# Gate products of seven mLSTM heads by Strassen's seven block products, in a part of their own

## The chip, the cores and the metric

The kernel runs on one core of a Trainium2 chip. The metric is device time in microseconds (us), the median of several executions. The core has a matrix engine (TensorE, PE in the profile), a vector engine (VectorE, DVE), a scalar engine (ScalarE, ACT), GpSimd (POOL), and a queue engine (SyncE, SP) that only issues transfers. Each works through its own list of instructions in order; semaphores connect them. Transfers run on 16 DMA engines that all queues share; here SP issues most of them, ACT and GpSimd a few.

## The reference, cut to what matters

A network of two layers works on 512 latent tokens and 256 context tokens, width 1024. Layer 0 mixes a long convolution with attention. Layer 1 is an mLSTM with 8 heads, and the change lies there. In short:

```
h            = rms_norm(x) * (1 + scale) + shift           # 768 x 1024
q, k, v, o, z, gates = split(h @ w_in)                     # per head: 128, 128, 256, 256, 256 columns
q, k         = silu(short_conv(q, k))
h_f, h_b     = chunkwise recurrence over q, k, v, gates, forward and backward
h            = rms_norm((h_f + h_b) * sigmoid(o), head_norm)
y            = (h * silu(z)) @ w_out                       # 512 latent tokens only
```

Of one head, o and z are needed for the 512 latent tokens alone, so their product is (512 x 1024) @ (1024 x 512). All numbers are fp32.

## The kernel before, in words

**Products.** The matrix engine takes a reduced fp32 form, so each fp32 operand is kept as two tiles, hi (a rounded copy, made by ACT) and lo (the rest, a subtraction on DVE). `split` (L1019) makes such a pair, and `mm3` (L1029) does one product as three matmuls: hi by hi, hi by lo, lo by hi. The activations of the layer lie in `hTh` and `hTl`, feature rows on the partitions, 8 feature tiles (`KT`) of 128 by 768 tokens. `load_w` (L1044) fetches a slice of 256 weight columns in two halves of 512 KB from SP into the three buffers `wr` and splits each half into `wh` and `wl`, which exist twice. `proj_tok` (L1196) then makes 128 tokens by 256 columns out of 8 x 3 = 24 matmuls; `proj_seg` (L1183) makes the transposed product for 512 or 256 tokens. Results lie in eight banks of PSUM, four called `pj`, four `pm`.

**Layer 1.** Head 0's values and the gate logits (`value`, L2347) come first, then `gates` (L2233), a chain of scans and exponentials on 64 rows, whose results `turn` (L2292) transposes. `head` (L2338) does a head: load the slice of q and k and that of v, project, convolve, apply silu (`conv_silu`, L2322), transpose the keys; then load the slices of o and z; then the recurrence over six chunks of 128 tokens, once forward and once backward (L2444 to L2504). Each step of the recurrence is a short chain: a matmul `pc`, an update of the state `C` on DVE, its split into `Ch` and `Cl`, a matmul with q, an addition on DVE. PE has other work in between: eight items, `out_gate` and `gate_z` (L2405 and L2411), 24 matmuls each, which `fill` places into the recurrence of the same head. `normed` and `result` (L2508 and L2521) finish a head and store it; they run inside the next one.

**The order.** Engine calls are not issued where they stand. `record` (L1004) collects them under a name, and `play` (L1009) issues them in the order that the table `ORDERS` gives for it, as numbers of recorded calls. What is issued so is pinned: every engine, SP and GpSimd included, goes through its calls in just this order (L1016, L1017). The parts that matter here are `l1a` (from head 0's values to `turn`) and `l1b` (the rest of layer 1, down to the first products of the output projection). `SLOTS` says in the same manner which buffer each tile takes. Nothing of `l1b` can be issued on an engine before its last call of `l1a`.

Of the kernel before, what the change touches and what calls it, by code (L numbers as in the profile page):

```python
# [7 lines left out]
F32 = mybir.dt.float32  # L8
# [6 lines left out]
P = 128  # L15
NL, NC, NT = 512, 256, 768
D = 1024
KT = 8
# [71 lines left out]
def _layout(i):  # L90
# [50 lines left out]
    o["head_norm"] = a["o_head_norm"][0].reshape(8, 1, 256)  # L141
# [10 lines left out]
class Ctx:  # L152
# [334 lines left out]
    ],  # L487
# [357 lines left out]
    ],  # L845
    "yraw@9": [
        1, 0, 0, 1, 1, 1, 0, 0,
    ],
    "ess@9": [
        0, 0, 0, 0, 0, 0,  # L850
# [1790 lines left out]
```

## Time and profile before

| | us |
|---|---|
| median of 3 runs (lowest, highest) | 1515.31 (1514.62, 1515.59) |
| the profiled execution | 1514.84 |
| its span, first to last instruction | 1513.1 |
| TensorE busy | 1480.6 |
| VectorE busy | 989.3 |
| ScalarE busy | 717.0 |
| GpSimd busy | 57.7 |

The span is what the profile shows; 1.74 us lie around it. A busy TensorE means that a matmul was under way; matmuls overlap, so a mean duration is longer than the distance from one start to the next. In groups and chains every instruction is put down to L1014, since the helper there issues all of them; the names of tiles tell them apart. In the rows of a window the columns are: the stretch, its length, busy time and number of instructions of PE, PEld, DVE, ACT and POOL, the granted TensorE clock, the busy share of the DMA engines, and GB/s.

### The profile page before, as it was taken

To read this page: it belongs to the slowest core of one execution; us is meant where nothing else is said; L and a number is where in the kernel's file an instruction comes from. 1 tells how busy PE (TensorE), PEld (TensorE's weight loads), DVE (VectorE), ACT (ScalarE), POOL (GpSimd) and SP (SyncE) were. 2 spreads that over 40 slices of the span, in tenths; PEclk is the share of its full clock that TensorE was granted. 3 is DMA by queue.
4 is the path that set the end of the run, shared out by engine and by line. 5 is a ranking of instruction groups with operands and counts; after the bars stand their busy time and mean duration, and the time that the engine had idled before them with its cause. 6 is when DMAs were issued, how large, how long until landed. Compare 5 with 4: busy or idle time off the path is not lost.

```text
span 1513.1 us, 25999 instructions
## 1 busy us (share of the span) xinstructions
PE 1480.6 (98%) x10542; PEld 1365.8 (90%) x10542; DVE 989.3 (65%) x1943; ACT 717.0 (47%) x1545; POOL 57.7 (4%) x97
## 2 busy tenths in 40 slices
PE   7999999999999999999999899999999999999997
PEld 5889999889999998989987789999999999999885
DVE  6688787887866666667236866666656575677435
ACT  6634344334434444445233667546354554546332
POOL 1000000000000000000000100000000000000000
PEclk9999999999999999999999999999999999999999
DMA  9411121221231111252643313131222323232741
GB/s 378 156 58 65 65 67 41 75 78 39 56 94 45 39 68 53 97 179 70 211 154 127 131 57 105 58 112 54 91 90 82 99 71 98 77 99 74 276 156 70
DMA packets 44815, 151.78 MB, mean 100 GB/s; under 512 B 5311, under 2 KB 7879, under 8 KB 42136
## 3 DMA queue, kind: packets, MB, share of 16 engines
q1 hardware_dynamic: 41448, 141.48, 28.2%
q0 software_dynamic: 1360, 6.42, 1.3%
q10 hardware_dynamic: 1888, 2.22, 0.5%
q8 instruction: 83, 1.36, 0.4%
q14 instruction: 36, 0.29, 0.1%
HBM read 135.39 MB, written 14.71 MB: 99 GB/s over the span
## 4 chain that ended last, share of the span: by engine, by line
PE 91%; DVE 3%; ACT 3%; issue 1%; DMA 1%; POOL 0%; SPq 0%; POOLq 0%; DVEq 0%; ACTq 0%
PE pj L1014 76%; PE pm L1014 13%; PE s L1014 3%; DVE wl L1014 0%; ACT hf L1014 0%; ACT wh L1014 0%; ACT q L1014 0%; DMA xt<-in_x 0%; DVE hf L1014 0%; DVE hh L1014 0%; DVE hTl L1014 0%; ACT wl L1014 0%; DVE yacc L1014 0%; DVE xt L1014 0%; ACT hTh L1014 0%
## 5 line engine op out<-in xcount | busy, mean ns | idle before, releaser
L1014 PE MATMUL pj<-wh,hTh 128*128 128x256 f32 (+2 forms) x1536 | 435.1, 289 | 5.1 <-ACT hTh L1014 1.9
L1014 PE MATMUL pj<-wl,hTh 128*128 128x256 f32 (+2 forms) x1536 | 433.0, 286 | 1.7 <-DVE wl L1014 1.7
L1014 PE MATMUL pj<-wh,hTl 128*128 128x256 f32 (+2 forms) x1536 | 430.1, 286 | 1.9 <-DVE hTl L1014 1.9
L1014 PEld LDWEIGHTS pj<-wh,hTh 128*128 128x128 f32 x1536 | 287.3, 189 | 12.0 <-ACT wh L1014 3.4
L1014 PEld LDWEIGHTS pj<-wl,hTh 128*128 128x128 f32 x1536 | 288.8, 189 | 4.8 <-DVE wl L1014 2.3
L1014 PEld LDWEIGHTS pj<-wh,hTl 128*128 128x128 f32 x1536 | 287.1, 189 | 4.2 <-DVE hTl L1014 2.1
L1014 PE MATMUL pj<-hTh,wh 128*128 128x512 f32 (+1 forms) x832 | 286.6, 345 | 0.0
L1014 PE MATMUL pj<-hTl,wh 128*128 128x512 f32 (+1 forms) x832 | 285.2, 343 | 0.6 <-DVE hTl L1014 0.6
L1014 PE MATMUL pj<-hTh,wl 128*128 128x512 f32 (+1 forms) x832 | 284.7, 343 | 0.0
L1014 DVE TENSOR_TENSOR wl<-wr,wh 128x1024 fp32r<-128x1024 f32 x149 | 180.5, 1214 | 75.0 <-ACT wh L1014 74.8
L1014 ACT CAST wh<-wr 128x1024 fp32r<-128x1024 f32 x149 | 154.2, 1044 | 81.6 <-PE pj L1014 41.9
L1014 PEld LDWEIGHTS pj<-hTh,wh 128*128 128x128 f32 x832 | 156.8, 188 | 18.5 <-ACT mrow L1014 0.4
L1014 PEld LDWEIGHTS pj<-hTh,wl 128*128 128x128 f32 x832 | 156.6, 188 | 18.7
L1014 PEld LDWEIGHTS pj<-hTl,wh 128*128 128x128 f32 x832 | 156.8, 188 | 17.9 <-DVE hTl L1014 0.9
L1014 DVE TENSOR_TENSOR PTl<-pj,PTh 128x384 fp32r<-128x384 f32 (+1 forms) x80 | 41.0, 525 | 21.5 <-ACT PTh L1014 21.4
L1014 ACT CAST PTh<-pj 128x384 fp32r<-128x384 f32 (+1 forms) x80 | 35.1, 459 | 41.1 <-PE pj L1014 38.7
L1014 DVE SCALAR_TENSOR_TENSOR C<-C,apb,pj 128x258 f32<-128x258 f32 x64 | 30.8, 481 | 33.7 <-PE pj L1014 27.5
L1014 DVE SCALAR_TENSOR_TENSOR cvo<-pj,cv,cvo 128x511 f32<-128x511 f32 (+1 forms) x48 | 31.2, 657 | 23.0 <-ACT cvo L1014 22.5
L1014 PE MATMUL pm<-Rh,dfa 128*128 128x256 f32 (+1 forms) x192 | 45.0, 305 | 0.0
L1014 DVE TENSOR_REDUCE mx<-s 128x1 f32<-128x768 f32 (+1 forms) x48 | 37.0, 773 | 11.2 <-PE s L1014 11.0
L1014 DVE TENSOR_TENSOR med<-big 128x512 f32<-128x512 f32 (+1 forms) x48 | 40.4, 865 | 5.0 <-ACT big L1014 4.8
L1014 PE MATMUL s<-dfa,qTh 128*128 128x256 f32 (+1 forms) x160 | 41.6, 342 | 1.3 <-ACT hdh L1014 1.3
(311 smaller groups left out, 2642.3 us busy)
## 6 DMA issues: line engine op xcount, KB each, us to landing
wr<-in_o_w_in SPq DMA_DIRECT2D x64, 512.0 KB, 4.8
wr<-in_e_w_in SPq DMA_DIRECT2D x52, 512.0 KB, 4.7
wh<-in_w_mod SPq DMA_DIRECT2D x18, 1024.0 KB, 5.1
wr<-in_e_w_out SPq DMA_DIRECT2D x16, 512.0 KB, 4.7
wr<-in_o_w_out SPq DMA_DIRECT2D x16, 512.0 KB, 6.6
xt<-in_x SPq DMA_DIRECT2D x12, 512.0 KB, 5.9
decay<-nc_scratch SPq DMA_DIRECT2D x16, 256.0 KB, 4.8
y_scratch<-y SPq DMA_DIRECT2D x8, 512.0 KB, 5.8
```

Source lines behind the costliest of these rows:

```text
L1014: x = fn(*a, **k)
```

## The change

For heads 0 to 6 the products for o and z move out of `head` into `l1a`, and are done by Strassen's scheme (Winograd's form). Of one head, the product (512 x 1024) @ (1024 x 512) is cut into 2 x 2 blocks: 256 tokens, 512 features, and o or z. Seven block products of 24 matmuls each take the place of eight. Five use sums of blocks:

- On the side of the activations the four forms `D1`, `F5`, `F6`, `F3` are made once for all heads: 4 additions of hi and lo (`whole`), 4 subtractions and 4 splits, each on 128 x 1024 numbers. Three products use plain blocks of `hTh` and `hTl`.
- On the side of the weights the sums are made anew for each head. A buffer `ch` (two exist) is loaded with one block and split; then GpSimd's queue issues a transfer that adds the next block to it, it is split again, and so on: four splits and three adding transfers, one after another. One more sum is made in a `wr` buffer (`r3`). So a head has 4 plain loads and 4 adding transfers of 512 KB, and 7 splits, where there were 4 loads and 4 splits.
- The results are put together on DVE and ACT, the tanh of both gates is applied, and the tiles are stored to DRAM (`ozd`), 512 KB each. The recurrence of the head loads them again, from SP.

The recurrence of head h now has the projections q, k and v of head h + 1 as its other work (`Head`); head 7 still has its own o and z, done the direct way. The multiplication of z by `head_norm` on DVE and the eight small loads of it on ACT's queue go; `result` scales by it while it copies out of PSUM. Tiles of `gates` share buffers with the new ones. The orders of `out0`, `l1a` and `l1b` and the slots are written anew.

The core of the diff:

```diff
+    A11, A12, A21, A22 = block(0, 0), block(0, 1), block(1, 0), block(1, 1)
+    a21, a11 = whole("zs", A21), whole("uu", A11)
+    V.tensor_tensor(a11, a21, a11, ALU.subtract)
+    D1 = form("d1", a11)
+    a22 = whole("so", A22)
+    V.tensor_tensor(a21, a21, a22, ALU.subtract)
+    F5 = form("f5", a21)
+    V.tensor_tensor(a22, a22, a11, ALU.subtract)
+    F6 = form("f6", a22)
+    a12 = whole("zs", A12)
+    V.tensor_tensor(a12, a12, a22, ALU.subtract)
+    F3 = form("f3", a12)
...
+    def product(ps, a, b):
+        for t in range(2):
+            for kt in range(4):
+                l = [x[:, kt, t * P:(t + 1) * P] for x in a]
+                out = ps[:, t * 256:(t + 1) * 256]
+                mm3(out, l, (b[0][:, kt], b[1][:, kt]), kt == 0, kt == 3)
+        return ps
+
+    def plus(raw, src):
+        G.dma_start(raw, src, accum_op=ALU.add)
...
+    def gates_oz(h):
+        o, z = ow[4 * h + 2], ow[4 * h + 3]
+        b11, b21, b12, b22 = o[:, 0:4], o[:, 4:8], z[:, 0:4], z[:, 4:8]
...
+        chain = raw_block(b11, "ch", 2, gp)
+        p1 = product(PJ(), A11, weights(chain))
+        S.copy(u, p1)
+        plus(chain, b12)
+        p2 = product(PM(), A12, weights(raw_block(b21)))
+        V.tensor_tensor(so[:, 0], p2, u, ALU.add)
+        S.activation(so[:, 0], so[:, 0], AF.Tanh, scale=0.5)
+        q5 = product(PJ(), F5, weights(chain))
+        plus(chain, b22)
+        r3 = raw_block(b12)
+        plus(r3, b22)
+        q7 = product(PM(), D1, weights(r3))
+        q6 = product(PJ(), F6, weights(chain))
+        plus(chain, b21)
+        V.tensor_tensor(u2, q6, u, ALU.subtract)
+        V.tensor_tensor(zs[:, 0], q5, u2, ALU.add)
+        V.tensor_tensor(u2, q7, u2, ALU.add)
+        V.tensor_tensor(zs[:, 1], q7, zs[:, 0], ALU.add)
+        q3 = product(PM(), F3, weights(raw_block(b22)))
+        V.tensor_tensor(zs[:, 0], q3, zs[:, 0], ALU.add)
+        q4 = product(PJ(), A22, weights(chain))
+        V.tensor_tensor(so[:, 1], q4, u2, ALU.subtract)
+        S.activation(so[:, 1], so[:, 1], AF.Tanh, scale=0.5)
+        for t in (1, 0):
+            th = T(gp, "gi", (P, 512))
+            S.activation(th, zs[:, t], AF.Tanh, scale=0.5)
+            V.scalar_tensor_tensor(zs[:, t], th, 1.0, zs[:, t], ALU.add, ALU.mult)
+        SP.dma_start(ozd[h, 0], so.rearrange("p t (i b) -> p (t i) b", b=256))
+        SP.dma_start(ozd[h, 1], zs.rearrange("p t (i b) -> p (t i) b", b=256))
+
+    for h in range(7):
+        gates_oz(h)
+        if h == 1:
+            turn()
+    play()
+    g1.close()
+    record("l1b")
...
+        if N:
+            N.load()
+            N.load_v()
+            SP.dma_start(so, ozd[h, 0])
+            SP.dma_start(zs, ozd[h, 1])
+            work = [(N.key, 0), (N.key, 1), (N.query,)] + [(N.value, i) for i in (4, 5, 0)] + [(N.turned,)] + [(N.value, i) for i in (1, 2, 3)]
...
-                S.copy(y[:, t], ps.rearrange("p n t -> p (n t)"))
+                S.activation(y[:, t], ps.rearrange("p n t -> p (n t)"), AF.Copy, scale=hnc[:, 2 * h + t:2 * h + t + 1])
```

In the new order of `l1a` the last calls are head 6's product `q4` (24 matmuls), then the subtraction that gives `so[:, 1]` (call 1708), its tanh (1709) and the store of `so` (1714). The new order of `l1b` begins with four of the five copies `ka` of head 0's first direction on ACT (calls 33, 35, 32, 36), the load of the first half of head 1's q and k weights on SP (3), and the four score products of head 0 on PE (21 to 24).

More of the change, by code (lines that the diff above doesn't have):

```diff
@@ new lines @@
+    "Ch@14": [
+        1, 0, 0, 1, 1, 0, 1, 0, 0, 1, 0, 1, 0, 1, 0, 1, 0, 1, 0, 0, 0, 1, 0, 0, 1, 0, 1, 0, 1, 0, 1, 0, 1, 0, 1, 0, 0, 1, 0, 1, 0, 1, 0, 1, 0, 1, 0,
+        1, 0, 1, 0, 1, 0, 1, 0, 1, 0, 1, 0, 1, 0, 1, 0, 1,
+    ],
+    "Cl@14": [
+        1, 0, 0, 1, 1, 0, 1, 0, 0, 1, 1, 0, 1, 0, 1, 0, 1, 0, 1, 1, 1, 1, 0, 0, 1, 1, 0, 1, 0, 1, 0, 1, 0, 1, 0, 1, 1, 0, 1, 0, 1, 0, 1, 0, 1, 0, 1,
+        0, 1, 0, 1, 0, 1, 0, 1, 0, 1, 0, 1, 0, 0, 1, 0, 1,
+    ],
+    "dn@14": [
+        0, 0, 0, 0, 0, 0, 0, 0, 0, 0, 0, 0, 0, 0, 0, 0,
+    ],
@@ L914 @@
+    "yraw2@15": [
+        0, 2, 3, 1, 0, 0, 1, 3,
+    ],
+    "ess@15": [
+        0, 0, 0, 0,
+    ],
+    "esst@15": [
+        0, 1, 0, 1,
+    ],
+    "ers@15": [
+        0, 1, 0, 1,
+    ],
+    "xt@15": [
+        2, 3, 0, 1,
     ],
@@ L2222, in _body @@
     S.dma_start(cv, ins["o_conv"])
+    hnc = T(mg, "hnc", (P, 16))
+    S.dma_start(hnc, ins["head_norm"])
     cq1 = T(mg, "cq1", (P, 6, P))
@@ L2233, in gates @@
     def gates():
-        g1 = ExitStack()
-        gp = g1.enter_context(pool("gates", side="right"))
         one, nil = ones[:64, 0, 0:1], ones[:64, 0, 1:2]
@@ L2306, in turn @@
             S.copy(cq2[:, :, 64:P], ps[:, :, 64:P])
-            play()
-            g1.close()
-            record("l1b")
-            return st.enter_context(pool("mr", side="right"))
         return turn
     first = {}
-    for tag, shape, dt, bufs in (("cvo", (P, NT), F32, 3), ("cvt", (P, NT), F32, 1), ("vh", (P, 6, 258), F32R, 2), ("vl", (P, 6, 258), F32R, 2)):
+    for tag, shape, dt, bufs in (("cvo", (P, NT), F32, 3), ("cvt", (P, NT), F32, 1), ("vh", (P, 6, 258), F32R, 1), ("vl", (P, 6, 258), F32R, 1)):
         first[tag] = T(mp, tag, shape, dt, bufs=bufs)
@@ L2334, in conv_silu, with __init__, value @@
         return out
-    state = []
-    def head(h, before):
-        vh = TM("vh", (P, 6, 258), F32R, 2)
-        vl = TM("vl", (P, 6, 258), F32R, 2)
-        G.memset(f(vh[:, :, 256:257]), 1.0)
-        G.memset(f(vh[:, :, 257:258]), 0.0)
-        G.memset(f(vl[:, :, 256:258]), 0.0)
-        kt_ = T(mp, "ktok", (P, 6, P))
-        def value(i):
+    class Head:
+        def __init__(self, h):
+            self.h = h
+            pl = mr if h % 2 else mp
+            self.vh, self.vl = (TM(t, (P, 6, 258), F32R) if h == 0 else T(pl, t, (P, 6, 258), F32R) for t in ("vh", "vl"))
+            G.memset(f(self.vh[:, :, 256:257]), 1.0)
+            G.memset(f(self.vh[:, :, 257:258]), 0.0)
+            G.memset(f(self.vl[:, :, 256:258]), 0.0)
+            self.qh, self.ql = (T(pl, t, (P, NL), F32R) for t in ("qh", "ql"))
+            self.pk = {}
+        def value(self, i):
+            h = self.h
             if h == 0 and values0:
-                ps, last = values0.pop(0), None
+                ps = values0.pop(0)
             else:
                 ps = PJ()[:, :288 if h == 0 else 256]
-                last = proj_tok(wv, i, ps)
-            split(vh[:, i, :256], vl[:, i, :256], ps[:, :256])
+                proj_tok(self.wv, i, ps)
+            split(self.vh[:, i, :256], self.vl[:, i, :256], ps[:, :256])
             if h == 0:
@@ L2384, in keys_turned @@
                 for c in range(nb):
-                    TE.transpose(ps[:, c], kk[:, (b0 + c) * P:(b0 + c + 1) * P], ident)
-                S.copy(kt_[:, b0:b0 + nb], ps[:, :nb])
-        if h == 0:
-            keys_turned()
-        for i in tiles:
-            last = value(i)
-            with behind(last):
-                if i == tiles[1]:
-                    keys_turned()
-                if before and i == 2:
-                    before.pop(0)()
-        so = T(mp, "so", (P, 4, 256))
@@ L2419, in head, with block @@
-        work = [(out_gate, i) for i in range(4)] + [(gate_z, i) for i in range(4)]
+                    TE.transpose(ps[:, c], self.kk[:, (b0 + c) * P:(b0 + c + 1) * P], ident)
+                S.copy(self.kt[:, b0:b0 + nb], ps[:, :nb])
+    gp = g1.enter_context(pool("gates", side="right"))
+    gt = T(gp, "wa", (P, 6, 4, 4, 8))
+    mr = None
+    H = Head(0)
+    H.wv = wv0
+    for i in (4, 5, 0, 1, 2, 3):
+        H.value(i)
+    def block(t, k):
+        return [x[:, 4 * k:4 * k + 4, 256 * t:256 * t + 256] for x in (hTh, hTl)]
@@ new lines, in form, with whole @@
+    def form(tag, src):
+        t = [T(gp, tag + x, (P, 4, 256), F32R) for x in "hl"]
+        split(t[0], t[1], src)
+        return t
+    def whole(tag, blk):
+        t = T(gp, tag, (P, 4, 256))
+        V.tensor_tensor(t, f(blk[0]), f(blk[1]), ALU.add)
+        return t
+    A11, A12, A21, A22 = block(0, 0), block(0, 1), block(1, 0), block(1, 1)
[3 more added lines that the diff above has]
+    a22 = whole("so", A22)
@@ new lines, in _body, with weights @@
+    V.tensor_tensor(a21, a21, a22, ALU.subtract)
[5 more added lines that the diff above has]
+    F3 = form("f3", a12)
+    turn = gates()
+    H.load()
+    for s in (1, 0):
+        H.key(s)
+    H.query()
+    H.turned()
+    forms = [0, None]
+    def weights(raw):
+        n = forms[0] % 2
+        if n == 0:
+            slot = wslot[0]
+            wslot[0] = 1 - slot
+            forms[1] = [wtile(f"w{x}{slot}", F32R) for x in "hl"]
+        forms[0] += 1
+        t = [x[:, 4 * n:4 * n + 4, :] for x in forms[1]]
+        split(t[0], t[1], raw)
+        return t
@@ new lines, in _body, with heads, out_gate, gate_z @@
+    for h in range(7):
[5 more added lines that the diff above has]
+    record("l1b")
+    mr = st.enter_context(pool("mr", side="right"))
+    def heads(h, H, N, before):
+        so = T(mr, "so", (P, 4, 256))
+        zs = T(mr, "zs", (P, 4, 256))
+        work = []
+        if N:
[4 more added lines that the diff above has]
+            work = [(N.key, 0), (N.key, 1), (N.query,)] + [(N.value, i) for i in (4, 5, 0)] + [(N.turned,)] + [(N.value, i) for i in (1, 2, 3)]
+        else:
+            wo = load_w(ow[4 * h + 2])
+            wz = load_w(ow[4 * h + 3])
+            def out_gate(i):
+                ps = PJ()[:, :256]
+                proj_tok(wo, i, ps)
+                S.activation(so[:, i], ps, AF.Tanh, scale=0.5)
+            def gate_z(i):
+                ps = PJ()[:, :256]
+                proj_tok(wz, i, ps)
+                S.activation(zs[:, i], ps, AF.Tanh, scale=0.5)
+                V.scalar_tensor_tensor(zs[:, i], zs[:, i], 1.0, ps, ALU.add, ALU.mult)
+            work = [(out_gate, i) for i in range(4)] + [(gate_z, i) for i in range(4)]
@@ L2421, in fill @@
         def fill():
             if work:
-                g, i = work.pop(0)
-                return g(i)
-        if h == 0:
-            for _ in range(4):
-                last = fill()
-            with behind(last):
-                state.append(turn())
-        mr = state[0]
+                g = work.pop(0)
+                g[0](*g[1:])
+        vh, vl, qh, ql, kk, qq, kt_ = H.vh, H.vl, H.qh, H.ql, H.kk, H.qq, H.kt
         decay = []
@@ L2496, in head @@
                 if c in (2, 4):
-                    last = fill()
+                    fill()
             late()
@@ L2504, in head @@
             den.append(dn)
+        while work:
+            fill()
         hh = T(mr, "hh", (P, 4, 256))
@@ L2535, in _body @@
     for h in range(8):
-        rest = head(h, rest)
-    raws = [T(mp, t, (P, n, NL), bufs=b) for t, n, b in (("vh", 3, 2), ("vl", 3, 2), ("cvo", 1, 3), ("cvo", 1, 3))]
+        N = Head(h + 1) if h < 7 else None
+        rest = heads(h, H, N, rest)
+        H = N
+    raws = [T(mp, t, (P, n, NL), bufs=b) for t, n, b in (("vh", 3, 1), ("vl", 3, 1), ("cvo", 1, 3), ("cvo", 1, 3))]
     k = 0
```

138 lines of the change are left out of this document (52 added, 86 removed), and 537 rows, old and new, of tables (ORDERS, SLOTS).

## The prediction

> **What bounds the kernel now.** I read the busy times first, then the chain of waits.
>
> ```profile
> span 1513.1 us, 25999 instructions
> PE 1480.6 (98%) x10542; PEld 1365.8 (90%) x10542; DVE 989.3 (65%) x1943; ACT 717.0 (47%) x1545; POOL 57.7 (4%) x97
> ...
> PE 91%; DVE 3%; ACT 3%; issue 1%; DMA 1%; POOL 0%; SPq 0%; POOLq 0%; DVEq 0%; ACTq 0%
> PE pj L1014 76%; PE pm L1014 13%; PE s L1014 3%; DVE wl L1014 0%; ACT hf L1014 0%; ACT wh L1014 0%; ACT q L1014 0%; DMA xt<-in_x 0%; DVE hf L1014 0%; DVE hh L1014 0%; DVE hTl L1014 0%; ACT wl L1014 0%; DVE yacc L1014 0%; DVE xt L1014 0%; ACT hTh L1014 0%
> ```
>
> TensorE sets the time: 98% of the span and 91% of the chain. A matmul less is time less, as long as nobody makes TensorE wait. So I looked at the stretches that the change touches, and at others where VectorE is fuller.
>
> ```profile
> core 0: us, PE busy (x) PEld busy (x) DVE busy (x) ACT busy (x) POOL busy (x), PEclk, DMA share, GB/s
> 200.00:400.00 200.00, 200.00 (x1260) 181.09 (x1259) 158.74 (x258) 84.81 (x137) 0.00 (x0) 1.00 0.20 63
> 320.00:340.00 20.00, 20.00 (x101) 16.71 (x100) 18.26 (x31) 6.19 (x8) 0.00 (x0) 1.00 0.23 68
> 360.00:380.00 20.00, 20.00 (x100) 16.70 (x101) 18.96 (x33) 7.31 (x10) 0.00 (x0) 1.00 0.02 8
> 680.00:700.00 20.00, 18.90 (x154) 17.12 (x153) 17.81 (x39) 15.13 (x29) 0.72 (x1) 1.00 0.27 93
> 860.00:876.00 16.00, 15.63 (x100) 15.60 (x101) 11.53 (x26) 8.33 (x18) 2.43 (x5) 0.81 0.41 132
> 876.00:916.00 40.00, 36.65 (x246) 33.36 (x245) 26.77 (x60) 30.63 (x54) 0.57 (x1) 1.00 0.31 83
> 990.00:1380.00 390.00, 389.94 (x2991) 376.32 (x2990) 247.47 (x506) 204.84 (x482) 17.04 (x34) 1.00 0.27 84
> 1420.00:1440.00 20.00, 20.00 (x175) 19.28 (x175) 4.25 (x5) 5.96 (x12) 0.00 (x0) 1.00 0.93 357
> ```
>
> The stretch from 876 to 916 us is the beginning of layer 1 (values of head 0, gates); TensorE stands still there for 40 - 36.65 = 3.35 us. The stretch from 990 to 1380 us is the steady run over heads: TensorE never stops, VectorE is busy for 247.47 / 390 = 63%. In the convolution stage, 200 to 400 us, VectorE is busy for 79% and TensorE still never stops; even 18.96 of 20 us did no harm there. At 680 to 700 us it did.
>
> **What a matmul is worth.** The distance from start to start, not the duration, is what a matmul costs in a full stretch:
>
> ```profile
> 1057.71 0.28 PE L1014 MATMUL pj<-wh,hTh 128*128 128x256 f32 x1
> ...
> 1058.19 0.28 PE L1014 MATMUL pj<-wl,hTh 128*128 128x256 f32 x1
> ```
>
> Four matmuls in 0.48 us: 0.120 us each. The change removes one block product of eight, 24 matmuls of this very shape, from seven heads: 168 x 0.120 = 20.2 us. All else on TensorE (projections of q, k, v, recurrence, transposes, head 7) keeps its count. Each block product costs 24 x 0.120 = 2.88 us, a head's seven 20.2 us, the new part 141 us.
>
> **What is added on VectorE and ScalarE.** Their durations:
>
> ```profile
> L1014 DVE TENSOR_TENSOR wl<-wr,wh 128x1024 fp32r<-128x1024 f32 x148 | 180.1, 1220 | 75.0 <-ACT wh L1014 74.8
> L1014 ACT CAST wh<-wr 128x1024 fp32r<-128x1024 f32 x148 | 153.9, 1049 | 80.6 <-PE pj L1014 41.0 <-PE pm L1014 33.6 <-DMA wr<-in_o_w_out 3.2
> L1014 DVE TENSOR_TENSOR yacc<-pj,yacc 128x512 f32<-128x512 f32 x30 | 20.4, 688 | 33.2 <-PE pj L1014 33.2
> L1014 DVE SCALAR_TENSOR_TENSOR zs<-zs,hn 128x256 f32<-128x256 f32 x32 | 13.4, 425 | 0.1
> L1014 DVE SCALAR_TENSOR_TENSOR zs<-zs,pj 128x256 f32<-128x256 f32 x32 | 13.2, 417 | 18.6 <-ACT zs L1014 18.4
> L1014 ACT ACTIVATE cvt<-cvo 128x512 f32<-128x512 f32 x6 | 3.8, 634 | 5.7 <-DVE cvo L1014 5.7
> L1014 ACT COPY y<-pm 128x512 f32<-128x512 f32 x12 | 7.0, 580 | 3.6 <-PE pm L1014 3.5
> ```
>
> In the new part a head takes on VectorE 7 x 1.22 for the splits and 9 x 0.69 for the sums of products: 14.7 us. On ScalarE it takes 7 x 1.05, one copy of 0.58 and four tanh of 0.63: 10.5 us. Both lie under 20.2 us of TensorE, 73% and 52%. I cost them at nothing in the middle of the part; at VectorE's 79% of the convolution stage that cover still held.
>
> At the *opening* it does not hold. The forms of the activations are 12 VectorE instructions of 128 x 1024, 14.6 us. Ahead of the first product that needs a form (`q5` of head 0), the written order has on VectorE 11 of these (13.4 us), 6 weight splits (7.3), and by the trace's own durations 4.1 us of head 0's values and logits, some 9 us of gate scans and 2.5 us of convolution: 36 us. TensorE has 29 us there (values 6.4, k and q of head 0 14.0, `q1`, `q2` 5.8, and small things). Seven us of standstill if VectorE works back to back and both start together; its busy time counts overlaps once, which by the row of 390 us takes some 8% off and leaves four. I take 5.0, with 3.35 (as now) and 8 as bounds.
>
> **The recurrence without its cover.** From 990 to 1380 us six heads pass, 65.0 us each, with 247.47 / 6 = 41.2 us of VectorE. Taking o and z out removes 192 x 0.120 = 23.0 us of TensorE and, on VectorE, 4 x 1.22 + 4 x 0.417 + 4 x 0.425 = 8.2 us. What is left is 42.0 us with 33.0 us of VectorE: 79%, just what the convolution stage carries at no loss. The recurrence is a chain of short steps, the other one is not; I take 1 us for all heads, bounds 0 and 18 (below).
>
> **The seam between the two lists.** Between `q4` of head 6, the last product of `l1a`, and head 0's recurrence, pinned orders leave TensorE little. The operations on the way are shown here and above:
>
> ```profile
> L1014 ACT ACTIVATE ka<-ktok,cq 128x128 f32<-128x128 f32 x80 | 29.6, 399 | 1.7 <-DVE kal L1014 1.5
> L1014 ACT CAST kah<-ka 128x640 fp32r<-128x640 f32 x16 | 11.7, 728 | 1.3 <-PE pj L1014 0.9
> y_scratch<-y SPq DMA_DIRECT2D x8, 512.0 KB, 5.8
> wr<-in_o_w_in SPq DMA_DIRECT2D x64, 512.0 KB, 4.8
> L1014 SPq DMA_DIRECT2D y_scratch<-y x8: 320/327/432, 985.3 to 1407.7; - x8
> ```
>
> After the last matmul (latency 0.28): the subtraction for `so` 0.69, its tanh 0.63. Only then does ScalarE come to its first call of `l1b`: five copies `ka` of 0.40, the cast `kah` 0.73. The state products can start 4.3 us after the last matmul; in between TensorE has the four score products, 0.4 us. So 3.9 us go. On SP the store of `so` waits for that tanh, and the load of head 1's first weights is queued behind it: 0.28 + 0.69 + 0.63, two issues of 0.33, 4.8 to landing, 1.05 for the cast is 8.1 us after the last matmul. The five state products (15 matmuls, 1.8 us) end at 6.1, so 2.0 us more go. The seam costs 5.9 us, with 3.9 (weights in time) and 8 (a landing of 5.8, as the stores have) as bounds. Whether the clock sinks with it: after waits of 1.9 us the row at 860 us shows 0.81, which is 0.19 x 16 = 3.0 us; from 876 to 916 us, with 3.35 us of standstill, it shows 1.00. I take 1.0.
>
> **The adding transfers.** No transfer of now adds. The nearest:
>
> ```profile
> PTl<-in_rope POOLq DMA_DIRECT2D x1, 512.0 KB, 4.8
> cs<-y_scratch POOLq DMA_DIRECT2D x2, 768.0 KB, 6.3
> dfb<-in_dft POOLq DMA_DIRECT2D x1, 768.0 KB, 11.5
> 671.38 0.75 POOL L1014 DMA_DIRECT2D dfb<-y_scratch  x1 [24.40 <-DVE gs L1014]
> ```
>
> Let L be the time to landing. A head's chain is one load (4.8), four splits (1.05 + 1.22 each, 9.1) and three adding transfers (issue 0.75 + L); two buffers `ch` let two heads overlap. With L = 4.8 the chain takes 30.5 us, 15.3 per head; with 6.3, 35.0 and 17.5; at L = 8.0 it takes 40.1, 20.1 per head, as much as the products. With 11.5 it is 50.6 and 25.3 per head, 36 us lost in seven. The first two are hidden by the products of the other head. The written order is closer than the mean, though: for head 6 about 7 us of TensorE work lie between the split that frees the buffer for the last sum and the product that uses it, and 2.3 us of these are the next split. I take L = 6.3 and 3.0 us lost, bounds 0 and 36. GpSimd's queue goes in order too: an adding transfer that waits holds up the other head's behind it. It has little else to do there, 57.7 us in the whole run.
>
> The Trainium skill (Collectives: The Full Stack, section "The bandwidth ceiling: the fold count and why AG ≠ RS ≠ AR") says that an addition inside a transfer needs two source reads, so that such a step ran at about half the rate of a plain copy; the adding itself costs nothing. No run here shows it yet. By that rule the moving part of a 512 KB transfer doubles: 524,288 bytes at the 357 GB/s of the row at 1420 us are 1.5 us, so L would be about 6.3 as an estimate, the value taken.
>
> Bytes: ten transfers of 512 KB per head in 20.2 us are 260 GB/s, against 84 GB/s in the steady run and 357 GB/s at a share of 0.93. Room is left, not much.
>
> **Costed at nothing.** The eight loads of `head_norm` and the multiplication by it on VectorE (32 x 0.425) lie under TensorE and only lower VectorE's load. The scaling copy in `result` has the copy's size (0.58). Loading `so` and `zs` back (2 x 512 KB per head) is needed a head later; without this cover it would cost 4.8 us per head.
>
> **The sum.** Against the profiled execution, 1514.84 us (span 1513.1 and 1.74 around it; 0.5 below the median): -20.2 for the matmuls, +5.0 opening, +5.9 seam, +1.0 clock, +3.0 adding transfers, +1.0 recurrence, -3.35 for the standstill that the opening has now. That is -7.65: **1507 us**. With the low bounds of all terms it is -20.2 + 3.35 + 3.9 - 3.35, 1498.5; with opening 6, seam 7, clock 2, transfers 4 and recurrence 1, 1511.3.
>
> **Rivals.** *The chain of adding transfers paces the part* (the slower side). Place: the four splits and three transfers of a head. It decides from L = 8.0 us on. With L = 9.6, twice the 4.8 of a plain one, the chain is 44.9 us, 22.5 per head, 2.3 too long in seven heads: 16 us in place of 3, **1520 us**; with 11.5, 1540. For it: the row of 11.5 us, the load on the DMA engines, the narrow order. Against it: 4.8 and 6.3 on this queue.
>
> *VectorE holds up the recurrence.* At 680 to 700 us, with 17.81 us of VectorE, TensorE lost 1.10 of 20 us. Over eight heads of 42 us that would be 18.5 us, 1524; if a third of the stretches go so, 6 us, **1513 us**, no change to be told. For it: the chains of the recurrence. Against it: 79% at no loss at 200 to 400 us.
>
> *Opening and seam at their upper bounds*, 8 and 8 us with 3.0 of lost clock at both: 1507 + 3 + 2.1 + 5 = **1517 us**, slower by a little.
>
> *It does not do what it says*: the count of matmuls must fall by 168, so nothing but standstill could eat the gain; that is the three above.
>
> **Chances.** The forecast 0.55 (its own range 1498 to 1511.5), paced by the transfers 0.23, recurrence held up 0.14, opening and seam 0.08. About 0.2%, 3.0 us, is what a measurement of this kernel can tell from no change, so faster means below 1511.8 and slower above 1517.9. Faster: the forecast and a small part of the second, 0.58. Same: most of the recurrence rival and part of the last, 0.16. Slower: 0.26. For 8 in 10 the range goes from 1496 (all hidden, and some standstill of now gone) to 1527, above the 1520 and 1524 of the rivals; beyond lies L near 11.5.
>
> **What would show each step.** In the profile after: 168 fewer matmuls, TensorE busy lower by about 20 us; in the opening waits of TensorE on VectorE for `d1`, `f5` or `wl`; one wait of some 4 us on `kah` and one on `wh` where the new part ends; waits of ScalarE on an addition into `ch`, and its time to landing, 6.3 or above 8; windows over the recurrence with VectorE at 79% and TensorE full. I am wrong if the new part runs for more than 22 us per head, if TensorE stands still for more than 5 us in the recurrence, or if the seam shows no wait.

## The result, and the profile after

The changed kernel is slower: 1530.98 us (median of four runs, 1528.37 to 1532.39) against 1515.45 (1514.62 to 1516.78), a ratio of 1.010 with the interval 1.0082 to 1.0117. The forecast was 1507, and the range ended at 1527. The profiled execution of the kernel after has a span of 1528.2 us, 15.1 more than before.

From the page of the kernel after: span, busy times, DMA queues (packets, MB, share of 16 engines' span) and chain of waits.

```profile
span 1528.2 us, 25907 instructions
PE 1476.9 (97%) x10374; PEld 1354.1 (89%) x10374; DVE 1047.4 (69%) x1979; ACT 746.2 (49%) x1549; POOL 82.1 (5%) x125
...
q1 hardware_dynamic: 45480, 156.16, 30.4%
q0 software_dynamic: 5392, 21.11, 7.1%
...
PE 26%; DVE 4%; DMA 3%; issue 2%; ACT 2%; POOL 0%; POOLq 0%; DVEq 0%; ACTq 0%; SPq 0%
```

From the page of the kernel before, the queue that GpSimd issues to:

```profile
q0 software_dynamic: 1360, 6.42, 1.3%
```

168 matmuls are gone (10542 to 10374), as predicted, but TensorE's busy time fell by 3.7 us only, from 1480.6 to 1476.9. The chain's 26% on TensorE can't be set beside the 91% of before: its shares add up to 37%, for it is followed back from the end to 942 us and no further. In that stretch transfers into `ch` hold 3% of the span, 41 us. The windows of the kernel after show where the time went (opening, first products, heads 1 to 3, heads 4 to 6, seam, recurrence; then four stretches by themselves):

```profile
core 0: us, PE busy (x) PEld busy (x) DVE busy (x) ACT busy (x) POOL busy (x), PEclk, DMA share, GB/s
876.00:905.00 29.00, 26.85 (x172) 24.31 (x173) 26.52 (x44) 18.50 (x27) 2.71 (x4) 1.00 0.54 129
905.00:925.00 20.00, 17.81 (x139) 16.75 (x138) 15.95 (x27) 12.82 (x18) 2.59 (x5) 1.00 0.72 137
925.00:1000.00 75.00, 73.54 (x596) 71.71 (x595) 51.40 (x66) 41.43 (x58) 11.18 (x14) 1.00 0.92 238
1000.00:1070.00 70.00, 58.76 (x423) 56.45 (x422) 36.74 (x44) 24.26 (x31) 7.80 (x10) 0.90 0.67 151
1070.00:1083.00 13.00, 8.72 (x36) 6.98 (x35) 6.10 (x8) 8.91 (x20) 0.64 (x1) 0.74 0.85 293
1083.00:1413.00 330.00, 327.88 (x2416) 310.46 (x2415) 255.42 (x545) 207.99 (x513) 20.79 (x43) 1.00 0.32 99
...
1007.40:1014.20 6.80, 5.83 (x25) 5.54 (x26) 1.23 (x1) 0.77 (x2) 1.72 (x2) 0.50 0.79 136
1075.70:1082.50 6.80, 5.78 (x20) 4.80 (x20) 4.06 (x5) 5.22 (x11) 0.64 (x1) 0.50 0.85 305
...
1031.30:1034.70 3.40, 3.40 (x18) 3.40 (x18) 1.99 (x3) 1.53 (x2) 0.10 (x1) 0.51 0.76 118
1434.10:1437.50 3.40, 3.07 (x13) 2.85 (x13) 1.41 (x2) 1.06 (x4) 0.00 (x0) 0.50 0.97 354
```

TensorE is idle for 2.15, 2.19, 1.46, 11.24, 4.28 and 2.12 us in these six stretches, 23.4 us together; before, it was idle for 3.4 us between 876 and 1398 us. Heads 4 to 6 lose most. The clock there is granted at 0.90, which is 7.0 of 70 us, and at the seam at 0.74, 3.4 of 13. The last rows show what this mean is made of: after pauses the clock stands at 0.50 for 6.8 or 3.4 us; in the first of these stretches 25 matmuls are done in a time that holds 57 at 0.120 each.

Busy time hides a part of the loss. Between 905 and 1070 us there are 139 + 596 + 423 = 1158 matmuls, nearly all of 128x256; at 0.120 us that is 139.0 us of 165, so 26.0 us are lost, where the idle time alone is 14.9. The rest is half clock, and the first matmul after each pause, which shows 0.28 us or more as busy where its due is 0.12. The Trainium skill (Perfetto Trace Analysis, section "Identifying the Most-Contended Engine") warns that busy time of pipelined matmuls is not a good measure of how well TensorE is used; this trace agrees, by the 11 us between those two numbers, though some 7 of them are half clock here.

One pause in the timeline of the kernel after (start, duration, engine; in brackets the idle time and what ended it), and the window from the issue of that addition to its landing:

```profile
996.64 0.85 POOL L999 DMA_DIRECT2D ch<-in_o_w_in  x1 [9.97 <-DVE wl L999]
...
1003.86 0.28 PE L999 MATMUL pm<-wh,f3l 128*128 128x256 f32 x1
...
1006.59 1.05 ACT L999 CAST wh<-ch 128x1024 fp32r<-128x1024 f32 x1 [4.24 <-DMA ch<-in_o_w_in]
...
1007.69 0.58 PE L999 MATMUL pj<-wh,f6h 128*128 128x256 f32 x1 [3.55 <-ACT wh L999]
```

```profile
996.60:1006.60 10.00, 7.54 (x64) 7.34 (x62) 3.15 (x3) 2.11 (x3) 1.70 (x2) 1.00 1.02 261
```

Head 4's addition ahead of product 6 is issued at 996.64 and lands 9.9 us later, at the cast's start. TensorE had run out of work at 1004.14. All 16 DMA engines are full in those 10 us (share 1.02), at 261 GB/s; before, a share of 0.93 moved 357.

Times to landing in the kernel after (last number, median):

```profile
wr<-in_o_w_in SPq DMA_DIRECT2D x57, 512.0 KB, 4.6
ch<-in_o_w_in POOLq DMA_DIRECT2D x21, 512.0 KB, 7.0
ch<-in_o_w_in SPq DMA_DIRECT2D x7, 512.0 KB, 8.9
wr<-in_o_w_in POOLq DMA_DIRECT2D x7, 512.0 KB, 9.5
```

The additions of the chain take 7.0 us, those for product 7 take 9.5, and even the plain load of a head's first block takes 8.9.

The seam, TensorE's rows in the timeline of the kernel after:

```profile
1069.46 0.28 PE L999 MATMUL pj<-wh,hTl 128*128 128x256 f32 x1
1069.58 1.05 PE L999 MATMUL pm<-cvo,cvo 128*128 128x128 f32 x8
1073.49 0.36 PE L999 MATMUL pj<-vh,kah 128*128 128x258 f32 x1 [2.86 <-ACT kah L999]
...
1077.62 1.01 PE L999 MATMUL pj<-hTh,wh 128*128 128x256 f32 x2 [1.02 <-ACT wh L999]
```

The last product ends at 1069.74, the first state product starts at 1073.49, and head 1's first product waits once more.

### The profile page after: what moved, and what is told of

Read it like the earlier page. It is cut to its first block, busy times and chain, and to the rows that moved or that the text cites. A ratio compares the mean times of both kernels' runs of the same rounds, so it can differ in the third digit from the quotient of the medians.

```text
span 1528.2 us, 25907 instructions
## 1 busy us (share of the span) xinstructions
PE 1476.9 (97%) x10374; PEld 1354.1 (89%) x10374; DVE 1047.4 (69%) x1979; ACT 746.2 (49%) x1549; POOL 82.1 (5%) x125
## 5 line engine op out<-in xcount | busy, mean ns | idle before, releaser
L999 PE MATMUL pj<-wh,hTh 128*128 128x256 f32 (+2 forms) x1200 | 343.3, 291 | 7.0 <-ACT wh L999 2.2
L999 PE MATMUL pj<-wl,hTh 128*128 128x256 f32 (+2 forms) x1200 | 342.0, 288 | 3.2 <-DVE wl L999 3.1
L999 PE MATMUL pj<-wh,hTl 128*128 128x256 f32 (+2 forms) x1200 | 340.4, 288 | 1.9 <-DVE hTl L999 1.9
L999 PEld LDWEIGHTS pj<-wh,hTh 128*128 128x128 f32 x1200 | 226.3, 190 | 13.9 <-issue 4.5
L999 PEld LDWEIGHTS pj<-wl,hTh 128*128 128x128 f32 x1200 | 227.3, 190 | 6.7 <-DVE wl L999 4.6
L999 PEld LDWEIGHTS pj<-wh,hTl 128*128 128x128 f32 x1200 | 226.3, 190 | 4.1 <-DVE hTl L999 2.1
L999 DVE TENSOR_TENSOR wl<-wr,wh 128x1024 fp32r<-128x1024 f32 x142 | 172.0, 1214 | 81.8 <-ACT wh L999 81.6
L999 PEld LDWEIGHTS pj<-hTl,wh 128*128 128x128 f32 x832 | 157.5, 189 | 18.2 <-DVE hTl L999 0.7
L999 DVE TENSOR_TENSOR wl<-ch,wh 128x1024 fp32r<-128x1024 f32 x28 | 34.1, 1222 | 24.0 <-ACT wh L999 23.8
L999 ACT COPY yacc<-pj 128x256 f32<-128x256 f32 x40 | 14.5, 374 | 63.8 <-PE pj L999 63.5
L999 ACT CAST wh<-ch 128x1024 fp32r<-128x1024 f32 x28 | 29.1, 1046 | 29.4 <-DMA ch<-in_o_w_in 17.8
```

Of the source, the lines that this page charges most:

```text
L999: x = fn(*a, **k)
```

## The experiments

The first theory (D) was that the DMA engines are the bound: additions keep them busy twice. Its rivals were C, that only the chain of a head's waits counts, and S, that opening, seam and recurrence cost the time.

**Plain in place of adding transfers.**

```diff
-        G.dma_start(raw, src, accum_op=ALU.add)
+        G.dma_start(raw, src)
```

> The 28 adding transfers become plain transfers of the same blocks on the same queue, with the same waits (the sums are not formed: products 5, 6, 7 and 4 use wrong blocks). Theory D (time of the DMA engines): an adding transfer keeps the engines busy twice as long per byte, so a head now needs 4 plain loads and 2 stores at 1.6 us of all engines and 4 adding ones at 3.2, 22.2 us, against 20.2 us of products; plain, it is 15.8 us. The share of the engines in the new part falls from 0.8-0.95 to about 0.6, TensorE's idle time there from 15 us to under 3, its clock there goes back to 1.00, and the time is 1512 us (1508 to 1517). Theory C (only the chain of a head's waits counts, not what else the engines carry): the landing of a block falls from 7.0 to about 4.7 us and the time is about 1513 too. Theory S (opening, seam and recurrence cost it): 1528 us or more.

Measured: 1524.4 us (1523.0 to 1529.41). Rows on landing, and the queue's share on the page; the profiled execution is the longest of the four, 1529.41 us:

```profile
ch<-in_o_w_in POOLq DMA_DIRECT2D x21, 512.0 KB, 4.9
ch<-in_o_w_in SPq DMA_DIRECT2D x7, 512.0 KB, 4.9
wr<-in_o_w_in POOLq DMA_DIRECT2D x7, 512.0 KB, 5.5
```

```profile
q0 software_dynamic: 5392, 21.11, 4.4%
```

Landing fell as both expected, 7.0 to 4.9, but at the median only 6.6 us came back where D and C said 18 or more. The same bytes on the same queue take 4.4 - 1.3 = 3.1% of the engines as copies and 7.1 - 1.3 = 5.8% as additions: 1.87 times. The rule of the Trainium skill quoted in the prediction (Collectives: The Full Stack, same section: two source reads, about half the rate) holds here, then, for the engines' time as well.

**Additions of 8 KB.**

```diff
-        G.dma_start(raw, src, accum_op=ALU.add)
+        G.dma_start(raw[:, 0:1, 0:16], src[:, 0:1, 0:16], accum_op=ALU.add)
```

> The adding transfers stay in their places with their waits, but each moves 128 x 16 elements, 8 KB in place of 512 (the sums are not formed but for that corner). It shows the part with nearly nothing of the adding left. Theories D and C: landing about 2 to 3 us, no waits in the part, 1510 us (1506 to 1515), not much under the plain transfers. Theory S: 1528 us or more.

Measured: 1517.8 us (1516.65 to 1520.56). Landing:

```profile
ch<-in_o_w_in POOLq DMA_DIRECT2D x21, 8.0 KB, 2.4
```

So the transfers cost 13.2 us in all. By the medians 6.6 go for the moving (4.9 against 2.4 to landing) and 6.6 for the adding (7.0 against 4.9), but the four times with plain transfers lie 6.4 us apart, so this division is rough. And without them the change still doesn't gain: 1517.8 against 1514.9 for the kernel before in the same comparison. Its windows for heads 1 to 3, for heads 4 to 6, and for the seam:

```profile
925.00:1000.00 75.00, 73.91 (x602) 72.20 (x601) 51.66 (x67) 41.25 (x59) 11.25 (x14) 1.00 0.54 158
1000.00:1057.00 57.00, 53.29 (x421) 51.87 (x420) 36.30 (x43) 23.97 (x31) 7.80 (x10) 0.97 0.32 100
1057.00:1070.00 13.00, 8.84 (x37) 7.26 (x37) 6.24 (x8) 8.64 (x19) 0.64 (x1) 0.74 0.75 257
```

1.1 us of idle stay in heads 1 to 3, 3.7 us of idle and 1.7 of clock (0.03 of 57) in heads 4 to 6; the seam is unchanged.

**Only product 7's addition cut down.**

```diff
-        plus(r3, b22)
+        plus(r3[:, 0:1, 0:16], b22[:, 0:1, 0:16])
```

> Only the adding into the block of product 7 (one of four per head, outside the chain of the other three) is cut down to 128 x 16 elements; product 7 then uses a wrong block. Theory D: the engines' time per head falls by 3.2 us from 22.2 to 19.0, under the 20.2 us of products; most of the loss goes, 1517 us (1512 to 1522). Theory C: the chain of three additions is as long as it was, 1528 to 1531 us.

Measured: 1527.66 us (1526.91 to 1530.66). D asked for 1517 and falls as the sole cause. The engines' load shows in the landing times (7.0 to 6.2 on the chain here), and the time came out as C has it, though C too had asked for 1513 of the plain transfers.

**One addition of four left.**

```diff
-        plus(chain, b12)
+        plus(chain[:, 0:1, 0:16], b12[:, 0:1, 0:16])
         ... the same for plus(chain, b22) and plus(r3, b22); plus(chain, b21) stays
```

> Only the last of the three additions of a head's chain (the one ahead of product 4) moves its 512 KB; the other three move 8 KB (the sums are not formed). It measures the time to landing of an adding transfer with few others beside it. If the addition itself is slow (its second read): 6 us or more, as against 4.6 to 4.9 for plain ones. If the 7.0 us of the kernel after come from the load on the DMA engines alone: 5 us or less.

Measured: 1520.32 us (one run). Landing:

```profile
ch<-in_o_w_in SPq DMA_DIRECT2D x7, 512.0 KB, 3.8
ch<-in_o_w_in POOLq DMA_DIRECT2D x7, 512.0 KB, 5.7
```

With few others beside it an addition takes 5.7 us, neither of the two expected ends: 1.9 more than a plain load here, and 1.3 less than among its like.

**The sums on GpSimd.**

```diff
-        G.dma_start(raw, src, accum_op=ALU.add)
+        G.tensor_tensor(raw, raw, src, ALU.add)
...
+        r12, r21, r22 = (T(wp, "wr", (P, 4, 256), bufs=3) for _ in range(3))
...
-        r3 = raw_block(b12)
-        plus(r3, b22)
+        SP.dma_start(r12, b12)
+        plus(r12, r22)
```

> The four sums of a head are made by GpSimd as plain additions in SBUF, from four blocks loaded once each (4 loads per head in place of 4 loads and 4 adding transfers); the loads stand earlier in the order. Theory L (what costs is the time from the issue of an addition to its landing, 0.85 + 7.0 us, three times in a row per head): GpSimd's select of 128 x 512 takes 0.81 us, so a sum of 128 x 1024 should take some 1.7 us, less than the 8 KB transfer's landing, and the time is that of the kernel with 8 KB transfers, 1518 us (1514 to 1522). Rival G (GpSimd's sums are slow or hold up VectorE): sums over 4 us or VectorE's 1.22 us splits longer by a fifth, 1525 us or more.

Measured: 1557.56 us (1557.48 to 1558.68). Groups of 905 to 1098 us there with a wait of 876 to 1100 us, and the splits of 905 to 1070 us in the kernel after:

```profile
L999 POOL TENSOR_TENSOR ch<-ch,wr 128x1024 f32<-128x1024 f32 x20 | 51.3, 2573 | 118.6 <-DVE wl L999 118.6
L999 DVE TENSOR_TENSOR wl<-ch,wh 128x1024 fp32r<-128x1024 f32 x27 | 38.9, 1451 | 15.0 <-ACT wh L999 15.0
...
ACT wh L999 <- DMA wr<-in_o_w_in: 18.2, 6, 7.9
```

```profile
L999 DVE TENSOR_TENSOR wl<-ch,wh 128x1024 fp32r<-128x1024 f32 x26 | 31.7, 1223 | 24.0 <-ACT wh L999 23.8
```

A sum takes 2.57 us, and VectorE's splits went from 1.22 to 1.45 us beside it, by 19%: rival G, near enough. It isn't the whole of the 27 us: the three blocks held for a head fill all three load buffers, and ScalarE waited 18.2 us for their loads. How much each took wasn't separated.

**A new seam.**

```diff
+    w1 = load_w(ow[4])
     play()
...
-            N.load()
+            if h:
+                N.load()
+            else:
+                N.w = w1
 order of "l1b": 18 of head 1's k products behind head 0's scores
```

> The adding transfers stay. Head 1's first weights are loaded and split at the end of the first list, before the stores of head 6's o and z, and 18 of its k products stand behind head 0's scores in the second list, so that TensorE has about 3 us of work while kah is made. Theory S2 (from the last product of the new part to a full TensorE 9 us are lost: 3.0 waiting for kah, the rest for weights and at half clock): 1523 us (1520 to 1526). Rival F (the fillers only move; the recurrence of head 0 then stands still later): 1528 us or more.

Measured: 1531.3 us (1528.84 to 1532.71), no gain. Two rows, SP's queue and TensorE:

```profile
1041.93 13.53 SPq L999 DMA_DIRECT2D wr<-in_o_w_in  x3
```

```profile
1088.15 0.38 PE L999 MATMUL pm<-Cl,qh 128*128 128x258 f32 x1 [1.94 <-DVE Cl L999]
```

Head 6's last load and the two early ones took 13.5 us to issue on SP, waiting for buffers, with the stores of heads 5 and 6 behind them. TensorE no longer waited for `kah`, but a pause of 1.94 us with half clock came later in head 0's recurrence, where the moved products had been: F for that part.

**Sums on GpSimd and new seam.** The edits of the last two, and head 6's first load earlier in the order.

> The sums on GpSimd and the new seam together; the load of head 6's first block also stands earlier. If the two losses add up (theories L and S2): 1510 us (1506 to 1514), under the kernel before. If either falls: 1517 us or more.

Measured: 1553.8 us (1552.55 to 1555.89), 3.8 us under the sums on GpSimd alone, with ranges apart. So the new seam or the earlier load gains there, which of the two isn't known, and the loss of the sums on GpSimd stays.

**Head 6's store of o on GpSimd's queue.**

```diff
-        SP.dma_start(ozd[h, 0], so.rearrange("p t (i b) -> p (t i) b", b=256))
+        (G if h == 6 else SP).dma_start(ozd[h, 0], so.rearrange("p t (i b) -> p (t i) b", b=256))
```

> The store of head 6's o is issued by GpSimd's queue instead of SP's, so that the load of head 1's first weights no longer stands behind it. By the prediction's own term for the seam the load lands 2.0 us earlier: 1529 us (1528 to 1530) under theories D and C. If the seam is worth more than its 5.9 us (theory S), up to 5 us less, 1526 us.

Measured: 1528.81 us (1526.18 to 1530.0), 2.2 less, near the prediction's term of 2.0; the ranges of the two kernels overlap. In its trace the wait of 1.02 us for `wh` at the seam is gone, the one of 2.86 us for `kah` stays.

**TensorE kept at work in its waits.** Finished groups of 12 matmuls are done again ahead of the waiting ones.

```diff
 order of "l1a", ahead of head 4's product 6:
+        second half of head 4's product 3, twice
 ahead of head 5's product 6 and head 6's product 5:
+        a finished half of a product of head 5 and of head 6, once
 "l1b": [ 33, 35, 32, 36, 3, 21, 22, 23, 24,
+         21, 22, 23, 24, eight times
```

> Every wait of the new kernel stays, but TensorE is kept at work in four of them: a group of 12 matmuls that is already done is done again once or twice ahead of the first matmul that waits (heads 4, 5 and 6), and head 0's four scores are done 8 times more at the seam. The same result. Theory K (a pause of some 2 us or more puts the clock at half for 3.4 or 6.8 us after it; that is 20.4 us at half between 1000 and 1083 us, worth up to 10 us): 1523 us (1520 to 1527), with the clock at 1.00 there. Rival (the waits alone cost, the clock nothing): 1531 us or more.

Measured: 1526.64 us (1525.61 to 1529.13). Windows of heads 4 to 6 and of the seam:

```profile
1000.00:1066.00 66.00, 60.48 (x488) 58.65 (x487) 37.48 (x44) 25.43 (x32) 7.80 (x10) 1.00 0.73 169
1066.00:1083.00 17.00, 16.38 (x118) 14.79 (x118) 6.65 (x9) 9.35 (x21) 1.09 (x2) 1.00 0.67 232
```

The clock is 1.00 throughout: the pauses had lowered it (theory K). The gain is 4.3 us, not the 10 that the half clock seemed worth, most likely because products that run faster wait longer for the next landing; this wasn't measured. With the scores repeated four times in place of eight:

```diff
-         21, 22, 23, 24, eight times
+         21, 22, 23, 24, four times
```

> The kernel in which TensorE is kept at work in four waits, with the scores at the seam repeated 4 times in place of 8: there the repeats had run 3 us longer than the wait for kah (first state product 7.8 us after the end of the last product, 3.8 without them). The same result. Theory K (clock): the wait is filled just to its end, no half clock, 1523 us (1521 to 1526). If the repeats weren't on the path, 1526 us or more.

Measured: 1525.9 us (1524.06 to 1527.6). It can't be told from the last, so the 3 us of overrun at the seam don't show in the time. In its profile one stretch at half clock is back in heads 4 to 6 (0.98 over 1000 to 1070 us).

**The end of the part and the seam mended, additions of 8 KB, and all of it with full additions.**

```diff
 order of "l1a": head 6's split for product 4 ahead of the tanh of z
 both stores of head 6: (G if h == 6 else SP).dma_start(...)
 order of "l1b": 21, 22, 23, 24 eight times more
 (the second kernel: full additions, and the repeats of heads 4 to 6)
```

> The kernel with 8 KB additions (the sums are not formed but for a corner), which took 1517.8 us, with three waits at the end of the new part taken away besides: the split for head 6's product 4 stands ahead of two tanh that wait for product 6; head 6's stores of o and z are issued by GpSimd's queue; head 0's four scores are done 8 times more, so that TensorE doesn't pause for kah. It bounds what is left of the change when the additions cost nothing. If the rest of the loss is the end of the part and the seam (2.3 us of waits and 1.7 of half clock at product 4, 2.0 for the store, about 3 of half clock behind the seam): 1510 us (1507 to 1514). If it is spread over the part and the recurrence: 1515 us or more.

Measured: 1517.77 us (1515.3 to 1518.88), no gain. TensorE's rows at the seam:

```profile
1056.35 8.20 PE L1000 MATMUL pm<-cvo,cvo 128*128 128x128 f32 x72
1064.30 0.36 PE L1000 MATMUL pj<-vh,kah 128*128 128x258 f32 x1
```

The repeats ran 8.2 us where the wait for `kah` had lasted 3.8 in the kernel after, so what was won behind the seam was paid ahead of it. This doesn't settle what the rest is.

> All additions as in the kernel after, with what helped put together: TensorE kept at work in three waits of heads 4 to 6 and at the seam (1526.6 us alone), head 6's two stores on GpSimd's queue (2.2 us alone), the split for head 6's product 4 ahead of the two tanh. If these add up: 1523 us (1520 to 1526), still over the kernel before. If the additions' landing takes their place: 1526 us or more.

Measured: 1529.72 us (1527.78 to 1532.33), no better than the repeats alone (1526.64); the ranges overlap. The pieces don't add up; which of the others takes the gain away wasn't tried.

**More VectorE in the recurrence.** The weights' subtractions done twice, or the values' three times.

```diff
 order of "l1b": each of the 28 subtractions wl of heads 1 to 7 twice in a row
```

> The kernel after, with each of the 28 subtractions that make the low parts of the next heads' q, k and v weights in the recurrence done twice (the same result): 34 us more of VectorE in 350 us, from 77% to 87%. If the recurrence has room on VectorE (it lost about 4 us against full TensorE): 1532 to 1537 us. If VectorE holds it up, as the second rival of the prediction has it: at least half of the 34 us, 1548 us or more.

```diff
 order of "l1b": each of the 42 subtractions vl of heads 1 to 7 three times in a row
```

> The kernel after, with each of the 42 subtractions that make the low parts of the next heads' values in the recurrence done three times (the same result): 35 us more of VectorE, as much as in the run that did the weights' subtractions twice (1548.0 us), but on results that are used only a head later. If it is VectorE's load that holds the recurrence up: again 1545 us or more. If it was the lateness of the weights: 1538 us or less.

Measured: 1548.02 us (1547.11 to 1549.76) and 1558.55 (1557.76 to 1559.67). The stores of the eight heads' y (first and last issue), in the kernel after, with the weights' and with the values' subtractions:

```profile
L999 SPq DMA_DIRECT2D y_scratch<-y x8: 319/323/433, 1133.8 to 1423.1; - x8
```

```profile
L1000 SPq DMA_DIRECT2D y_scratch<-y x8: 319/323/435, 1137.7 to 1442.7; - x8
```

```profile
L1002 SPq DMA_DIRECT2D y_scratch<-y x8: 319/323/432, 1134.3 to 1451.1; - x8
```

From first to last store 289.3 us became 305.0 and 316.8. Of 34 us added, 17 show in the time; of 35, 28. The recurrence has little room on VectorE for work in these places, though it is busy there for 255.42 / 330 = 77% and TensorE for 99%. The second run was to take the weights' lateness out, and it cost more; but these subtractions also free the values' PSUM banks, so load and lateness aren't cleanly separated.

No version that computes the whole beats the kernel before; the best is at 1525.9 us. A new order of `l1a` that leaves each sum more room wasn't tried.

## Why the prediction was wrong

Term by term (idle time from the windows above, clock as (1 - granted) x length):

| term | predicted | shown |
|---|---|---|
| 168 matmuls | -20.2 | -20.2 |
| standstill of now | -3.35 | gone: -3.35 |
| opening | +5.0 | 2.15 + 2.19 = +4.3 |
| middle of the part | 0 | 1.1 + 3.7 + 1.7 = +6.5, with additions of 8 KB |
| adding transfers | +3.0 | +13.2 |
| seam | +5.9 | +4.3 |
| clock | +1.0 | +3.4 at the seam |
| recurrence | +1.0 | +2.1 |

The right column adds up to +10.2; the spans differ by 15.1. The other 4.9 us weren't assigned; a part lies under busy time, in the first matmuls after pauses. The half clock from 1434 us on isn't counted: it lies behind the last store of y, and from there to the end both kernels take the same time (1407.7 to 1513.1 before, 1423.1 to 1528.2 after).

**The matmuls** were right in number and price, **the opening** and **the seam** within their bounds. In the seam the parts came out nearly too: the first state product starts 4.0 us after the last matmul's start (1069.46 to 1073.49; predicted 4.3), with 2.86 us of standstill (predicted 3.9), then comes a wait for `wh` of 1.02, where 2.0 were predicted.

**The adding transfers** are the step that failed most: 3.0 predicted, 13.2 measured, 10.2 of the 24.0 us between 1507 and 1531. Three choices of the prediction were wrong in it.

First, the landing. L = 6.3 was near the price of an addition with few beside it (5.7), but the load was counted once per byte ("260 GB/s, room is left"). Counted in engine time, by the shares of the profile pages, an addition weighs 1.87: four plain loads, two stores and four additions are 4 + 2 + 4 x 1.87 = 13.5 transfers a head in place of 10. The engines were then 92% busy from 925 to 1000 us, and every landing grew: to 7.0, 9.5, and 8.9 for a plain load.

Second, the test "decides from L = 8.0" took the mean of two overlapping chains. It passes over the written order: for each sum, the matmuls that stand in the list between the split that frees the block (for product 7, the addition itself) and the first product that uses the sum. Counted in the order, at 0.120 us each, these distances go from 5.2 to 11.5 us (and one 28.8). A sum needs about 0.3 to the issue, L, and 1.05 for the cast: 8.4 us at L = 7.0, 6.3 at 4.9, 3.8 at 2.4. Of the 28 distances 12 are shorter than the first, 4 than the second, none than the third, in the order of the three times measured: 1531.0, 1524.4, 1517.8. Three points in order don't prove the count, and place by place the median doesn't tell where TensorE waits: the two longest waits for a sum, 3.55 us for head 4's product 6 and 1.70 for head 5's, stand at distances of 9.0 and 9.2 us. There the additions took 9.9 and 9.7 us to land, so a sum needed about 11. Distance and landing have to be set against each other for each place; why the landing differs so from place to place stays open. The prediction had such a number for head 6 ("about 7 us", less 2.3 for the next split; counted in this way it is 9.2) and still went by the mean. The rival named the right place, but would have left this kernel alone at L = 7.0.

Third, the price of a pause. A wait was counted once. It can count again as half clock: the pause of 3.55 us at 1007.69 is followed by 6.8 us at 0.50. The clock term stood for the seam alone, with the mean of 0.81 from the row at 860 us as its measure; the granted clock of a window is a mean over full and half. The Trainium skill (TensorE: Matmul & The Clock Gate, section "Part 1: The HAM clock gate (the "warmup" mystery)") knows two states, half and full, and windows of about 3.4 us. The trace agrees in the 0.50 and in lengths of 3.4 and 6.8 us. It asks for an idle window of 3.4 us ahead of the fall, and here the measurement differs. These are the pauses of TensorE ahead of the half clock at 1031.3 us:

```profile
1026.02 0.39 PE L999 MATMUL pm<-wl,d1h 128*128 128x256 f32 x1 [0.37 <-DVE wl L999]
...
1029.06 0.38 PE L999 MATMUL pj<-wh,f6h 128*128 128x256 f32 x1 [1.70 <-ACT wh L999]
...
1030.32 0.38 PE L999 MATMUL pj<-wl,f6h 128*128 128x256 f32 x1 [0.88 <-DVE wl L999]
```

None is as long as 3.4 us; 2.95 us of idle within 5 were enough. Nor does the length alone decide: at 877 us a pause of 1.70 us in the kernel after is followed by no half clock, and one of 1.78 us at the same place, in the run with product 7's addition cut down, is. The stretch behind it, in the kernel after and in that run:

```profile
877.70:881.10 3.40, 3.40 (x28) 3.40 (x27) 3.37 (x5) 0.74 (x2) 0.00 (x0) 1.00 0.02 5
```

```profile
877.70:881.10 3.40, 3.40 (x17) 3.38 (x16) 3.37 (x5) 0.66 (x2) 0.00 (x0) 0.52 0.02 5
```

So a part of the spread between executions of one kernel can be the clock.

**The middle of the part**, costed at nothing under 73% of VectorE, lost 6.5 us. With additions of 8 KB TensorE waits there for splits of heads 4 to 6, one after another, in the written order. The share of busy time was no cover for an order that makes a split just in time. That the place of the splits is the cause wasn't tested by itself: the run that moved one of them also overran at the seam.

**The recurrence** was priced about right (1.0 against 2.1), but for a wrong reason. "79%, just what the convolution stage carries at no loss" took two stages with the same share for alike. The two runs with more VectorE show that this one has little room: of each us added, 0.5 to 0.8 us shows. The rival's mechanism is there; at this kernel's load it costs 2.1 us at most.

The signs that the prediction named for being wrong did appear for the part: 165 us for seven heads, 23.6 us per head, over the 22 named. For the recurrence (5 us) and the seam (no wait) they did not.

## What to carry to other kernels

Price a transfer that adds at nearly two in DMA-engine time, and see what it does to the landing of all others, not only to its own. Test a written order place by place: for each transfer, the work that stands between what frees its buffer and what uses it, against issue, landing and cast; a mean per round shows nothing. And where TensorE is dense, reckon with half clock behind pauses that come to some 2 us within 5, though not every time, and judge its fill by matmuls times their start-to-start distance, not by busy time.

## What the runs showed of the hardware that was not expected

- A 512 KB addition from GpSimd's queue lands in 5.7 us with few transfers beside it (plain load 3.8), in 7.0 to 9.5 among its like, and takes 1.87 times the DMA engines' time of a copy on the same queue.
- In the stretches looked at, the clock is granted at 1.00 or 0.50, the latter for 3.4 or 6.8 us. It fell after three pauses of 2.95 us together, none longer than 1.70, and after one of 1.78 in one run, but not after one of 1.70 in another. Repeating finished matmuls in the waits kept it at 1.00 from 1000 to 1083 us and took 4.3 us off the kernel (1531.0 to 1526.6).
- GpSimd's sum of 128x1024 takes 2.57 us, and stretches VectorE's splits beside it from 1.22 to 1.45 us.
- An engine at 77% busy can have little room left: 35 us more of VectorE in the recurrence cost 28.
